# Group B of an attention block: where the score differences live, and when the fp16 pieces are made

## The chip, the cores and the metric

One core of a Trainium2 chip runs the kernel in one launch. The metric is the device time of that launch in microseconds (us). Engines: PE (TensorE matmul; PEld is its weight load), DVE (VectorE), ACT (ScalarE), POOL (GpSimd) and SP (SyncE), which here issues the DMAs. SBUF is the working memory; PSUM is the memory into which matmuls write.

## The reference

One layer, sequence 1024, width 1024, float32:

```python
n = rms_norm(h, norm1_g)
qa, ka, va, qb, kb, vb = split(n @ w_in)
ya = mixer_a(qa, ka, va, sinks)      # 8 heads of 64, 2 K/V heads, window of 3 chunks of 64, ALiBi, sinks
yb = mixer_b(qb, kb, vb, rel_bias)   # 8 heads of 64, own chunk and 8 chunks before it
y = concat(rms_norm(ya, g_a), rms_norm(yb, g_b))
h = h + y @ w_out
h = h + square(relu(rms_norm(h, norm2_g) @ w_ff1)) @ w_ff2
out = rms_norm(h, final_norm_g)
```

mixer_b, which the change touches, is per head: `scores = q k^T / 8 + bias[clipped distance]` over the nine chunks of the band (a key outside it counts -1e30), `softmax` over them, times v.

## The kernel before, in words

The program first projects the first K, Q and V of group A, then does group A's attention, group B's, the output projection with the second norm, and the MLP. Every fp32 product is made from a high and a low piece of its operands.

**Group B.** Queries go in row blocks of 128, keys likewise; row block i sees key blocks max(0, i − 4) to i, so n = 128 to 640 columns. Heads come in pairs j = 0 to 3 (`Pair("B", j, ...)`). A `UnitB` is one head of a pair (s = 0, 1) for one half of the sequence (t = 0, 1; four row blocks). The order is, for each pair, (s0, t0), (s1, t0), (s0, t1), (s1, t1): 16 units, 64 calls of `score`. In units of t = 0 the row blocks have 128, 256, 384 and 512 columns, in units of t = 1 all have 640.

`score(b)` of row block b does, in this order:
- PE: the scores into PSUM tile S (two banks; two such tiles);
- DVE (L554): bias − score, with the row minimum into nm, written back into S. The page calls it CUSTOM_DVE_ANT_0; a second small instruction reads the minimum;
- ACT (L555): the exponential in place in S, with the row sum into sm;
- DVE (L764, L765): scale and reciprocal of the sum, rc;
- ACT (L770): the high fp16 piece, S × rc, into H (SBUF; two such tiles);
- DVE (L771): the low fp16 piece, S × rc − high, into the same H;
- SP (L772): a DMA that transposes H into G (fp16, one per unit; three such tiles, one of pool `at` and two of pool `atB`).

`step`/`apply` of a unit multiplies G by V, key block by key block, into PSUM tile av; a unit of t = 0 has four such steps and needs all four row blocks at the first, one of t = 1 has eight and needs row block 0 at the first, 0 and 1 at the second, and so on. After the last step ACT copies av out (L802, L803), and at s = 1 POOL adds the halves and `finish` makes y.

**Order.** The calls of `score` run two units ahead: while unit u is applied, `interleave` puts the four calls of `score` of unit u + 2 between its steps, and between those `Filler` steps of three matmuls each: the projections of the pairs to come (ip_kB, ip_qB, ip_vB) and at last the output projection of group A's part (op_A). PE's order is fixed by hand in the order of the calls. On the other engines and in the queue of SP, a planner at compile time orders the instructions by its own times and by when tiles come free; each engine then runs its list strictly in that order.

**Biases.** `Pair.biases()` is called in each `score`; its first call in a pair loads both heads' biases (L590, 320 KB each, two tiles `bias`) on SP and has POOL fill two corners of each with -1e30 (L591, L592).

**Pools.** `atA` (six P tiles of group A, 640 columns of fp32) is closed at the first unit of group B, and `atB` (two G tiles) is opened over it. Pool `at` has the biases, three PT tiles, H, one G tile and Y.

Of the kernel before, what the change touches and what calls it, by code (L numbers as in the profile page):

```python
# [17 lines left out]
P = 128  # L18
# [34 lines left out]
def kernel(  # L53
# [61 lines left out]
    small.tile([P, 88], F32, tag="pad", bufs=1, name="pad")  # L115
# [425 lines left out]

    def exponentials(kind, i, bias, init, S, pr, nm, sm):

        k0, n = window(kind, i)
        w = (2 if kind == "A" else 5) * P
        bs = bias[:, w - n : w]
        if kind == "A":
            S, pr = S[:, 0, :n], pr[:, :n]
        elif n > 512:
            S, bs = S[:, :, :320], bs.rearrange("p (a b) -> p a b", a=2)  # L550
            pr = S
        else:
            S = pr = S[:, 0, :n]
        nc.vector.tensor_tensor_reduce(pr, S, bs, -1.0, init, ALU.add, ALU.min, nm)  # L554
        nc.scalar.activation(pr, pr, AF.Exp, bias=nm, scale=-1.0, accum_out=sm)  # L555
        return k0, n, pr
# [12 lines left out]
    class Pair:  # L569
# [7 lines left out]
        def biases(self):  # L577
            if self.kind == "A" and self.j == 0:
                return first_bias
            if self.bias:  # L580
                return self.bias
            for s in range(2):
                h = 2 * self.j + s
                b = at.tile([P, 5 * P], F32, tag="bias", bufs=2, name=f"b_{self.kind}{h}")
                if self.kind == "A":
                    far = b[:, 2 * P : 4 * P]
                    nc.sync.dma_start(far, dist)
                    nc.gpsimd.tensor_scalar(b[:, : 2 * P], far, 2.0 ** -(h + 1), None, ALU.mult)
                else:
                    nc.sync.dma_start(b, relb[h])  # L590
                    nc.gpsimd.memset(b[:HD, 5 * P - HD :], NEG)  # L591
                    nc.gpsimd.memset(b[HD:, :HD], NEG)  # L592
                self.bias.append(b)
            return self.bias

# [57 lines left out]
    class UnitA:  # L653
# [10 lines left out]
        def score(self, s):  # L664
# [4 lines left out]
            pt = atA.tile([P, 5 * P], F32, tag="P", bufs=6, name=f"P_{self.name}_{s}")  # L669
# [21 lines left out]
        def turn(self, u):  # L691
# [4 lines left out]
            T = self.T[u] = at.tile([P, 2, HALF], F32R, tag="PT", bufs=3, name=f"T_{self.name}_{u}")  # L696
# [41 lines left out]
    units_b = [0]  # L738

    class UnitB:  # L740


        def __init__(self, pair, s, t):
# [5 lines left out]
            self.at = {}  # L749

        def score(self, b):
            p, h = self.pair, self.h
            if b == 0:
                self.nm, self.sm, self.rc = stats(self.name)
                bank = banks_of_b()
                n = units_b[0] % 3
                units_b[0] += 1
                pool, bufs = (at, 1) if n == 0 else (group_ps[2], 2)
                self.G = pool.tile([P, 40, P], F16, tag="T16", bufs=bufs, name=f"G_{self.name}")
            c = slice(b, b + 1)  # L760
            S = group_ps[1].tile([P, 2, 512], F32, tag="S", bufs=2, name=f"S_{self.name}_{b}")
            scores("B", self.i0 + b, p.Q[self.s], p.K[self.s :: 2], S)
            k0, n, q = exponentials("B", self.i0 + b, p.biases()[self.s], BIG, S, None, self.nm[:, c], self.sm[:, c])
            nc.vector.tensor_scalar(self.sm[:, c], self.sm[:, c], 2.0**-P_UP, None, ALU.mult)  # L764
            nc.vector.reciprocal(self.rc[:, c], self.sm[:, c])  # L765
            H = at.tile([P, 10 * P], F16, tag="P16", bufs=2, name=f"H_{self.name}_{b}")
            hi, lo = H[:, :n], H[:, n : 2 * n]
            if n > 512:
                hi, lo = (v.rearrange("p (a b) -> p a b", a=2) for v in (hi, lo))
            nc.scalar.activation(hi, q, AF.Copy, scale=self.rc[:, c])  # L770
            nc.vector.scalar_tensor_tensor(lo, q, self.rc[:, c], hi, ALU.mult, ALU.subtract)  # L771
            nc.sync.dma_start_transpose(self.G[:, 10 * b : 10 * b + 2 * n // P], H[:, : 2 * n])  # L772
            self.at[self.i0 + b] = (10 * b - k0, n // P)
# [175 lines left out]
    for j in range(4):  # L949
# [4 lines left out]
        pair = Pair("B", j, Q, K, V, y7 if j == 3 else None)  # L954
        units += [(UnitB(pair, s, t), f"B{j}", B_FILL[4 * j + 2 * t + s]) for t in range(2) for s in range(2)]
# [18 lines left out]
    for unit, name, n_fill in units:  # L974
# [7 lines left out]
        nexts = list(look_ahead(LOOK_AHEAD))  # L982
        interleave(unit, nexts, n_fill, unit.name[0] == "A" and ahead and ahead[-1].name[0] == "B")
# [566 lines left out]
```

## Time and profile before

| | |
|---|---|
| median of 3 runs | 1107.96 us (1103.93 to 1111.24) |
| the profiled execution | 1105.94 us |
| its span, first to last instruction | 1103.7 us |
| granted TensorE clock, mean | 0.983 |
| PE busy | 1038.9 us |
| DVE, ACT, POOL busy | 674.2, 599.2, 429.9 us |
| first score of group B, last product with V | 156.9 us, 425.0 us |

The profile gives for a group of instructions its line, engine, operation, tiles (`out<-in`), shapes and count, then busy us, mean ns of one, and the idle time of the engine just before them with what ended it. A row of waits reads: who waited, for what, us in total, how often, the longest. A row of the timeline reads: start us, length, engine, line, operation, and in brackets the idle time before it and its releaser. A matmul's line is always that of a helper (L165), so products are told apart by their tiles: S_B scores of group B, av_B products with V, op_A the output projection.

### The profile page before, as it was taken

How to read it: one execution, taken by the hardware profiler on the slowest of the kernel's cores; microseconds unless marked ns; L12 is line 12 of the kernel's file. 1: busy time of each engine (PE TensorE's matmuls, PEld its weight loads, DVE VectorE, ACT ScalarE, POOL GpSimd, SP SyncE). 2: the span in 40 equal slices, each digit the busy share in tenths (PEclk: the TensorE clock that was granted, in tenths of full speed). 3: DMA queues.
4: the chain of work that ended last, by engine and by line, in shares of the span. 5: the costliest groups of instructions: out<-in, count | busy, mean ns of one | idle time of the engine just before them, and what ended most of it. 6: DMA issues, size and time to landing. Idle time of an engine off the chain costs nothing.

```text
span 1103.7 us, 14073 instructions
## 1 busy us (share of the span) xinstructions
PE 1038.9 (94%) x4787; PEld 834.9 (76%) x4787; DVE 674.2 (61%) x1108; ACT 599.2 (54%) x1005; POOL 429.9 (39%) x334
## 2 busy tenths in 40 slices
PE   9999988987687987999999999999999999999997
PEld 7888876756455655888888888888888888888885
DVE  6578765646454362588543244334888776778666
ACT  8677776635475584767545444545623333333346
POOL 0567783322352343502644443454114124024125
PEclk9999998999899998999999999999999999999999
DMA  9945456896999678232545354235898545533004
GB/s 359 247 115 149 138 145 161 164 209 121 218 224 261 142 165 253 109 106 94 184 153 177 110 172 172 110 120 210 312 390 311 167 134 170 174 115 96 1 1 153
DMA packets 146119, 187.98 MB, mean 170 GB/s; under 512 B 79744, under 2 KB 97152, under 8 KB 146048
## 3 DMA queue, kind: packets, MB, share of 16 engines
q1 hardware_dynamic: 145904, 186.83, 56.4%
q8 instruction: 38, 0.62, 0.2%
q14 instruction: 33, 0.27, 0.1%
q10 hardware_dynamic: 144, 0.26, 0.1%
HBM read 105.26 MB, written 45.09 MB: 136 GB/s over the span
## 4 chain that ended last, share of the span: by engine, by line
PE 63%; ACT 1%; DVE 1%; DMA 0%; issue 0%; POOL 0%; ACTq 0%; DVEq 0%
PE f L165 28%; PE f_a L165 16%; PE f_c L165 8%; PE op_B L165 4%; PE f_b L165 4%; PE op_A L165 1%; PE tp L168 1%; PE av_B L165 1%; DMA G_B<-H_B 0%; PE S_B L165 0%; ACT H_B L770 0%; DVE H_B L771 0%; PE end L165 0%; ACT yc L803 0%; PE ss_B L165 0%
## 5 line engine op out<-in xcount | busy, mean ns | idle before, releaser
L165 PE MATMUL f<-X,W 128*128 128x512 f32 x1344 | 311.3, 393 | 0.0
L165 PEld LDWEIGHTS f<-X,W 128*128 128x128 f32 x1344 | 252.1, 188 | 57.9 <-DVE X L171 0.4
L165 PE MATMUL f_a<-V,U 128*128 128x512 f32 x756 | 174.9, 390 | 0.0
L171 POOL TENSOR_TENSOR U<-u,U 128x1024 fp32r<-128x1024 f32 x32 | 79.3, 2480 | 230.9 <-PE f_c L165 137.2
L165 PEld LDWEIGHTS f_a<-V,U 128*128 128x128 f32 x756 | 141.9, 188 | 31.1 <-DVE C L1439 0.3
L171 POOL TENSOR_TENSOR W<-T,W 128x1024 fp32r<-128x1024 f32 x29 | 75.5, 2604 | 144.9 <-ACT W L1146 140.2
L165 PE MATMUL S_B<-KkB,QqB 128*128 128x320 f32 (+2 forms) x192 | 48.4, 363 | 43.7 <-DVE H_B L771 37.1
L165 PE MATMUL f_c<-V,U 128*128 128x512 f32 x384 | 89.0, 390 | 0.0
L165 PEld LDWEIGHTS f_c<-V,U 128*128 128x128 f32 x384 | 72.1, 188 | 15.6
L1146 ACT ACTIVATE V<-Z 128x1024 fp32r<-128x1024 f32 x32 | 33.9, 1059 | 90.4 <-PE f_a L165 45.3
L165 PEld LDWEIGHTS S_B<-KkB,QqB 128*128 128x128 f32 x192 | 31.7, 199 | 55.0 <-issue 37.9
L771 DVE SCALAR_TENSOR_TENSOR H_B<-S_B,rc_B,H_B 128x640 f16<-128x640 f32 (+2 forms) x64 | 45.7, 716 | 44.0 <-ACT H_B L770 43.8
L1146 ACT ACTIVATE V<-w 128x1024 fp32r<-128x1024 f32 x24 | 25.5, 1061 | 81.6 <-issue 34.8
L171 DVE TENSOR_TENSOR V<-w,V 128x1024 fp32r<-128x1024 f32 x24 | 50.2, 2090 | 31.0 <-ACT V L1146 31.0
L171 POOL TENSOR_TENSOR W<-w,W 128x1024 fp32r<-128x1024 f32 x23 | 56.4, 2456 | 32.1 <-ACT W L1146 32.0
L1195 DVE TENSOR_TENSOR k<-f,k 128x1024 f32<-128x1024 f32 x24 | 29.3, 1222 | 63.7 <-PE f L165 63.7
L555 ACT ACTIVATE S_B<-S_B,nm_B 128x640 f32<-128x640 f32 (+2 forms) x64 | 40.4, 632 | 49.8 <-DVE nm_B L554 47.4
L1146 ACT ACTIVATE U<-u 128x1024 fp32r<-128x1024 f32 x56 | 58.6, 1046 | 10.3 <-DMA ud<-k 6.5
L554 DVE CUSTOM_DVE_ANT_0 S_B<-S_B,b_B 128x640 f32<-128x640 f32 (+2 forms) x64 | 42.3, 664 | 34.6 <-PE S_B L165 19.7
L770 ACT ACTIVATE H_B<-S_B,rc_B 128x640 f16<-128x640 f32 (+2 forms) x64 | 42.0, 659 | 37.3 <-DMA G_B<-H_B 25.1
L1189 ACT ACTIVATE k<-f 128x1024 f32<-128x1024 f32 x24 | 24.6, 1026 | 62.2 <-PE f L165 62.2
L165 PE MATMUL ip_qB<-nT,w_qB 128*128 128x512 f32 x192 | 53.6, 413 | 0.9 <-DVE ts_kB L359 0.9
(247 smaller groups left out, 1981.7 us busy)
## 6 DMA issues: line engine op xcount, KB each, us to landing
w<-in_w_ff_dram SPq DMA_DIRECT2D x64, 512.0 KB, 4.8
u<-ud SPq DMA_DIRECT2D x56, 512.0 KB, 4.4
ud<-k SPq DMA_DIRECT2D x48, 512.0 KB, 3.0
KkB<-ts_kB SPq DMA_DIRECT2D x64, 128.0 KB, 2.3
yd<-y SPq DMA_DIRECT2D x14, 512.0 KB, 3.2
y<-yd SPq DMA_DIRECT2D x14, 512.0 KB, 6.3
xr<-in_x_dram SPq DMA_DIRECT2D x8, 512.0 KB, 8.6
QqB<-ts_qB SPq DMA_DIRECT2D x32, 128.0 KB, 2.3
```

The costliest lines, as they stand in the source:

```text
L165: pe(nc.tensor.matmul(*args, **kw))
L168: pe(nc.tensor.transpose(*args))
L171: return engine.tensor_tensor(lo, full, f(hi), ALU.subtract)
L554: nc.vector.tensor_tensor_reduce(pr, S, bs, -1.0, init, ALU.add, ALU.min, nm)
L555: nc.scalar.activation(pr, pr, AF.Exp, bias=nm, scale=-1.0, accum_out=sm)
L770: nc.scalar.activation(hi, q, AF.Copy, scale=self.rc[:, c])
L771: nc.vector.scalar_tensor_tensor(lo, q, self.rc[:, c], hi, ALU.mult, ALU.subtract)
L1146: nc.scalar.activation(w[0], full, AF.Copy)
L1189: nc.scalar.activation(kept[p], ps, AF.Copy)
L1195: dve.tensor_tensor(v, ps, v, ALU.add)
```

## The change

- The difference (L554) is written into P, a tile in SBUF (640 columns of fp32, three in pool `at`), no longer back into S; exponential, high and low piece read P. Group A's P tiles are three of `at` and three of `atA`, in turn.
- The pieces of two row blocks are made together and later. `score(b)` first puts the scores on PE, then runs one item of the list `defer`, then makes difference and exponential. After odd b two items are appended for the pair (b − 1, b): `upper` (scale and reciprocal for both columns at once, both high pieces) and `lower` (both low pieces, both transposes). So `upper` runs in the next call of `score`, `lower` in the one after it; for blocks 2 and 3 these are calls of the next unit. What is left is run when no scores are left to come, and before a unit's first product with V.
- H has three tiles. G has two tiles for units of t = 0 (26 columns of 128 each, in `at`) and two for t = 1 (40 columns, in `atB`).
- Biases: unit (s0, t0) loads its pair's second bias in call 1 and fills its corners in call 3; unit (s1, t1) does this for the next pair's first. Pair 0 loads and fills both in its own first call.
- `atA` has the PT tiles now; it is closed, and `atB` opened, at the first unit of t = 1. The small tile `pad` has 8 columns, no longer 88.

```diff
-    small.tile([P, 88], F32, tag="pad", bufs=1, name="pad")
+    small.tile([P, 8], F32, tag="pad", bufs=1, name="pad")
...
-            group_ps.append(ap_.enter_context(tc.tile_pool(name="atB", bufs=1, reuse_waits="tile")))
...
-    atA = group_ps[0].enter_context(tc.tile_pool(name="atA", bufs=1, reuse_waits="tile"))
+    only_a = ExitStack()
+    atA = only_a.enter_context(tc.tile_pool(name="atA", bufs=1, reuse_waits="tile"))
+    only_b = []
+
+    def pool_of_b():
+        if not only_b:
+            only_a.close()
+            only_b.append(ap_.enter_context(tc.tile_pool(name="atB", bufs=1, reuse_waits="tile")))
+        return only_b[0]
+
+    rows_of_a = [0]
+
+    def tile_of_a(name):
+        n = rows_of_a[0]
+        rows_of_a[0] += 1
+        pool, bufs = (atA, 3) if n % 2 else (at, 3)
+        return pool.tile([P, 5 * P], F32, tag="P", bufs=bufs, name=name)
...
-        if kind == "A":
-            S, pr = S[:, 0, :n], pr[:, :n]
-        elif n > 512:
-            S, bs = S[:, :, :320], bs.rearrange("p (a b) -> p a b", a=2)
-            pr = S
+        pr = pr[:, :n]
+        if n > 512:
+            v = lambda a: a.rearrange("p (a b) -> p a b", a=2)
+            nc.vector.tensor_tensor_reduce(v(pr), S[:, :, :320], v(bs), -1.0, init, ALU.add, ALU.min, nm)
         else:
-            S = pr = S[:, 0, :n]
-        nc.vector.tensor_tensor_reduce(pr, S, bs, -1.0, init, ALU.add, ALU.min, nm)
+            nc.vector.tensor_tensor_reduce(pr, S[:, 0, :n], bs, -1.0, init, ALU.add, ALU.min, nm)
         nc.scalar.activation(pr, pr, AF.Exp, bias=nm, scale=-1.0, accum_out=sm)
...
             for s in range(2):
+                if self.kind == "B":
+                    self.load_bias(s)
+                    self.mask_bias(s)
+                    continue
...
+        def load_bias(self, s):
+            h = 2 * self.j + s
+            b = at.tile([P, 5 * P], F32, tag="bias", bufs=2, name=f"b_B{h}")
+            nc.sync.dma_start(b, relb[h])
+            self.bias.append(b)
+
+        def mask_bias(self, s):
+            b = self.bias[s]
+            nc.gpsimd.memset(b[:HD, 5 * P - HD :], NEG)
+            nc.gpsimd.memset(b[HD:, :HD], NEG)
...
-            pt = atA.tile([P, 5 * P], F32, tag="P", bufs=6, name=f"P_{self.name}_{s}")
+            pt = tile_of_a(f"P_{self.name}_{s}")
...
-            T = self.T[u] = at.tile([P, 2, HALF], F32R, tag="PT", bufs=3, name=f"T_{self.name}_{u}")
+            T = self.T[u] = atA.tile([P, 2, HALF], F32R, tag="PT", bufs=3, name=f"T_{self.name}_{u}")
...
-    units_b = [0]
+    defer, pairs_b = [], []
...
             if b == 0:
                 self.nm, self.sm, self.rc = stats(self.name)
-                bank = banks_of_b()
-                n = units_b[0] % 3
-                units_b[0] += 1
-                pool, bufs = (at, 1) if n == 0 else (group_ps[2], 2)
-                self.G = pool.tile([P, 40, P], F16, tag="T16", bufs=bufs, name=f"G_{self.name}")
+                banks_of_b()
+                pool, cols = (pool_of_b(), 40) if self.t else (at, 26)
+                self.G = pool.tile([P, cols, P], F16, tag=f"T16_{self.t}", bufs=2, name=f"G_{self.name}")
             c = slice(b, b + 1)
             S = group_ps[1].tile([P, 2, 512], F32, tag="S", bufs=2, name=f"S_{self.name}_{b}")
+            pt = at.tile([P, 5 * P], F32, tag="P", bufs=3, name=f"P_{self.name}_{b}")
             scores("B", self.i0 + b, p.Q[self.s], p.K[self.s :: 2], S)
-            k0, n, q = exponentials("B", self.i0 + b, p.biases()[self.s], BIG, S, None, self.nm[:, c], self.sm[:, c])
+            if defer:
+                defer.pop(0)[1]()
+            self.P[b] = exponentials("B", self.i0 + b, p.biases()[self.s], BIG, S, pt, self.nm[:, c], self.sm[:, c])
+            if b % 2:
+                self.next_bias(b == 1)
+            if b % 2:
+                H = {}
+                defer.append((self, lambda: self.upper(b - 1, H)))
+                defer.append((self, lambda: self.lower(b - 1, H)))
+
+        def next_bias(self, load):
+            s, j = 1 - self.s, self.pair.j + self.s
+            if self.s != self.t or j in (0, 4):
+                return
+            if load:
+                pairs_b[j].load_bias(s)
+            else:
+                pairs_b[j].mask_bias(s)
+
+        def upper(self, b0, H):
+            c = slice(b0, b0 + 2)
             nc.vector.tensor_scalar(self.sm[:, c], self.sm[:, c], 2.0**-P_UP, None, ALU.mult)
             nc.vector.reciprocal(self.rc[:, c], self.sm[:, c])
-            H = at.tile([P, 10 * P], F16, tag="P16", bufs=2, name=f"H_{self.name}_{b}")
...
-            nc.scalar.activation(hi, q, AF.Copy, scale=self.rc[:, c])
-            nc.vector.scalar_tensor_tensor(lo, q, self.rc[:, c], hi, ALU.mult, ALU.subtract)
-            nc.sync.dma_start_transpose(self.G[:, 10 * b : 10 * b + 2 * n // P], H[:, : 2 * n])
-            self.at[self.i0 + b] = (10 * b - k0, n // P)
+            for b in (b0, b0 + 1):
+                k0, n, q = self.P[b]
+                H[b] = at.tile([P, 10 * P], F16, tag="P16", bufs=3, name=f"H_{self.name}_{b}")
+                nc.scalar.activation(H[b][:, :n], q, AF.Copy, scale=self.rc[:, b : b + 1])
+
+        def lower(self, b0, H):
+            for b in (b0, b0 + 1):
+                k0, n, q = self.P[b]
+                nc.vector.scalar_tensor_tensor(
+                    H[b][:, n : 2 * n], q, self.rc[:, b : b + 1], H[b][:, :n], ALU.mult, ALU.subtract
+                )
+                o = (10 if self.t else 6) * b
+                nc.sync.dma_start_transpose(self.G[:, o : o + 2 * n // P], H[b][:, : 2 * n])
+                self.at[self.i0 + b] = (o - k0, n // P)
...
             if first:
+                while any(q[0] is self for q in defer):
+                    defer.pop(0)[1]()
...
         nexts = list(look_ahead(LOOK_AHEAD))
+        while defer and not nexts:
+            defer.pop(0)[1]()
```

More of the change, by code (lines that the diff above doesn't have):

```diff
@@ L582, in biases @@
             for s in range(2):
+                if self.kind == "B":
+                    self.load_bias(s)
+                    self.mask_bias(s)
+                    continue
                 h = 2 * self.j + s
                 b = at.tile([P, 5 * P], F32, tag="bias", bufs=2, name=f"b_{self.kind}{h}")
[L585 to L592, printed above, removed]
+                far = b[:, 2 * P : 4 * P]
+                nc.sync.dma_start(far, dist)
+                nc.gpsimd.tensor_scalar(b[:, : 2 * P], far, 2.0 ** -(h + 1), None, ALU.mult)
                 self.bias.append(b)
             return self.bias
+        def load_bias(self, s):
[7 more added lines that the diff above has]
+            nc.gpsimd.memset(b[HD:, :HD], NEG)
         def rows(self, t):
@@ L748, in __init__ @@
             self.second = [lambda n=n: self.step(n) for n in range(len(self.kbs))]
-            self.at = {}
+            self.at, self.P = {}, {}
         def score(self, b):
@@ L954 @@
         pair = Pair("B", j, Q, K, V, y7 if j == 3 else None)
+        pairs_b.append(pair)
         units += [(UnitB(pair, s, t), f"B{j}", B_FILL[4 * j + 2 * t + s]) for t in range(2) for s in range(2)]
```

3 lines of the change are left out of this document (removed).

## The prediction

> **What bounds the kernel now.** I read the page's busy shares first, then busy time by stretch (columns: length, then busy us and count of PE, PEld, DVE, ACT and POOL, granted clock, DMA share, GB/s), cut where group B's first score and the last group B product lie.
>
> ```profile
> PE 1038.9 (94%) x4787; PEld 834.9 (76%) x4787; DVE 674.2 (61%) x1108; ACT 599.2 (54%) x1005; POOL 429.9 (39%) x334
> 0.00:156.00 156.00, 154.15 (x808) 129.25 (x809) 110.78 (x316) 118.82 (x311) 90.69 (x106) 1.00 0.63 190
> 156.00:290.00 134.00, 113.59 (x543) 86.29 (x542) 76.15 (x214) 75.93 (x147) 49.61 (x63) 0.96 0.79 172
> 290.00:412.00 122.00, 96.28 (x456) 68.21 (x455) 59.21 (x170) 74.26 (x149) 45.77 (x50) 0.94 0.85 202
> 412.00:426.00 14.00, 4.84 (x18) 2.40 (x17) 2.56 (x5) 6.42 (x13) 8.34 (x13) 0.63 1.07 310
> 426.00:1103.70 677.70, 670.06 (x2970) 548.79 (x2968) 425.48 (x405) 323.74 (x388) 235.50 (x104) 1.00 0.45 157
> ```
>
> TensorE bounds the whole, but not evenly. Before 156 us and after 426 us it is all but full at clock 1.00. In the 270 us of group B it is busy 113.59 + 96.28 + 4.84 = 214.7 us, so 55.3 us are idle, and only there can this change act. Next, PE's waits and its longest gaps in the timeline:
>
> ```profile
> PE S_B L165 <- DVE H_B L771: 37.1, 17, 7.6
> PE av_B L165 <- DMA G_B<-H_B: 9.2, 2, 7.5
> PE S_B L165 <- DVE sm_B L764: 5.3, 5, 1.7
> 166.32 0.98 PE L165 MATMUL S_B<-KkB,QqB 128*128 128x384 f32 x2 [4.05 <-DVE H_B L771]
> 264.62 1.29 PE L165 MATMUL S_B<-KkB,QqB 128*128 128x320 f32 x4 [3.89 <-DVE H_B L771]
> 298.87 0.98 PE L165 MATMUL S_B<-KkB,QqB 128*128 128x384 f32 x2 [7.62 <-DVE H_B L771]
> 355.39 1.40 PE L165 MATMUL S_B<-KkB,QqB 128*128 128x320 f32 x4 [4.83 <-DVE H_B L771]
> 419.67 0.80 PE L165 MATMUL av_B<-G_B,VvB 128*128 128x384 f16 x2 [7.47 <-DMA G_B<-H_B]
> ```
>
> A score product waits for the low piece H (L771) of the row block two calls earlier: that is the last reader of its PSUM tile S, which has two buffers. This costs 37.1 + 5.3 = 42.4 us. Of the 17 waits on L771 four make 20.4 us; the other thirteen average 1.3 us. The 9.2 us stand at the end of the stage, where the last unit's transposes must land.
>
> Why L771 is late, in DVE's and ACT's waits:
>
> ```profile
> DVE H_B L771 <- ACT H_B L770: 43.8, 37, 3.7
> DVE sm_B L764 <- ACT S_B L555: 33.6, 42, 2.1
> DVE S_B L554 <- POOL b_B L591: 13.3, 2, 8.9
> ACT H_B L770 <- DMA G_B<-H_B: 25.1, 17, 3.7
> ```
>
> DVE and ACT hand each block back and forth, ACT also waits for an H buffer that a transpose still reads, and twice the first difference of a pair waits for its bias; the longer of these, 8.9 us, is what ends in the 7.62 us gap.
>
> **The change, part by part.** The durations at the widest block (640 columns), the same operations where they already use SBUF (group A's P_A, and y), and last the start of the first difference (164.1):
>
> ```profile
> L554 DVE CUSTOM_DVE_ANT_0 S_B<-S_B,b_B 128x640 f32<-128x640 f32 x32 | 26.6, 830 | 11.3 <-PE S_B L165 11.1
> L554 DVE DVE_READ_ACCUMULATOR2_ANT nm_B<- 128x1 f32 x64 | 9.1, 142 | 0.0
> L555 ACT ACTIVATE S_B<-S_B,nm_B 128x640 f32<-128x640 f32 x32 | 24.5, 764 | 15.9 <-DVE nm_B L554 13.8 <-DVE sm_B L764 2.0
> L555 ACT ACTIVATION_READ_ACCUMULATOR S_B<-S_B,nm_B 128x1 f32 x64 | 12.5, 195 | 0.0
> L764 DVE TENSOR_SCALAR sm_B<-sm_B 128x1 f32<-128x1 f32 x64 | 9.7, 152 | 34.3 <-ACT S_B L555 33.6
> L765 DVE RECIPROCAL rc_B<-sm_B 128x1 f32<-128x1 f32 x64 | 10.4, 163 | 1.9
> L770 ACT ACTIVATE H_B<-S_B,rc_B 128x640 f16<-128x640 f32 x32 | 25.4, 792 | 18.3 <-DMA G_B<-H_B 7.8 <-DVE nm_B L554 3.8 <-issue 2.8
> L771 DVE SCALAR_TENSOR_TENSOR H_B<-S_B,rc_B,H_B 128x640 f16<-128x640 f32 x32 | 28.2, 882 | 18.4 <-ACT H_B L770 18.4
> L554 DVE CUSTOM_DVE_ANT_0 P_A<-S_A,b_A,nsink 128x256 f32<-128x256 f32 x56 | 25.2, 479 | 4.9 <-PE S_A L165 4.7
> L554 DVE CUSTOM_DVE_ANT_0 S_B<-S_B,b_B 128x256 f32<-128x256 f32 x8 | 3.5, 439 | 1.1 <-PE S_B L165 1.1
> L555 ACT ACTIVATE P_A<-P_A,nm_A 128x256 f32<-128x256 f32 x56 | 28.1, 503 | 12.0 <-DVE nm_A L554 11.9
> L555 ACT ACTIVATE S_B<-S_B,nm_B 128x256 f32<-128x256 f32 x8 | 3.5, 443 | 3.1 <-DVE nm_B L554 3.1
> L771 DVE SCALAR_TENSOR_TENSOR H_B<-S_B,rc_B,H_B 128x512 f16<-128x512 f32 x8 | 6.0, 748 | 6.6 <-ACT H_B L770 6.6
> L816 DVE SCALAR_TENSOR_TENSOR y<-Y,gain_vB,y x8: 743/752/1177, 219.9 to 428.7; 128x512 fp32r<-128x512 f32 x8
> L554 DVE CUSTOM_DVE_ANT_0 S_B<-S_B,b_B x64: 289/756/833, 164.1 to 409.8; 128x640 f32<-128x640 f32 x32, 128x128 f32<-128x128 f32 x8, 128x256 f32<-128x256 f32 x8, 128x384 f32<-128x384 f32 x8
> ```
>
> *Early release of S.* Now a PSUM tile is held for 0.83 + 0.14 + 0.76 + 0.20 + 0.15 + 0.16 + 0.79 + 0.88 = 3.9 us after its score. 64 calls over 214.7 us are 3.4 us a call, so PE wants the tile back 6.7 us later, less 0.7 us for the score: about 2 us of slack, and every delay beyond that stops PE. Afterwards PE needs only the difference: 0.97 us, slack 5 us. The next ring is P, three SBUF tiles: the difference of block 3 takes the tile of block 0, and stands on DVE behind the pair's two low pieces. The loop from block 1's difference is 0.97 + 0.96 + 0.31 + two high pieces 1.58 + a low piece 0.88 + 0.97 = 5.7 us, and PE asks for the result four calls (13.4 us) later: slack 7 us. So some 3 us are gained on every wait. That erases the thirteen short ones and leaves about 1 and 2 us of those of 3.89 and 4.83.
>
> *Biases one unit ahead.* The same eight loads and sixteen small fills, moved ahead on SP and POOL. Three calls (10 us) lie between load and use, and a bias lands in 3.3 to 5.2 us (below), so the 7.62 us go. The very first pair still loads both at once: its first difference starts at 164.1 us and S is free by 164.5 instead of 166.3, so of 4.05 us some 2 stay. On POOL a fill can stand behind another wait; then the difference and the score two calls on wait too. I keep that in the remainder.
>
> *Cost of SBUF.* Exponent: 503 against 443 ns, 0.06 × 64 = 4 us more on ACT. Difference: 479 against 439, 2.5 us on DVE. The high piece's price from SBUF at this width stands in no row; between nothing and the exponent's 0.06, I take 0.03, so 2 us more of ACT. Scale and reciprocal go from 64 to 32 each: DVE saves 32 × 0.315 = 10 us. All this is hidden as long as ACT (75.93 + 74.26 + 6.42 = 156.6 us now, 163 then) keeps room in a stage of some 239 us: 68%.
>
> *Low piece with two SBUF inputs.* y (L816) already has this form: its median of 752 ns equals the 748 ns from PSUM, its longest is 1177. I take no extra cost. The Trainium skill, page "SBUF — State Buffer", section "Who interferes with whom", says that a VectorE instruction with two SBUF inputs contends with a GpSimd instruction that reads SBUF; the median of L816 doesn't show it, its maximum may. If each of the 64 paid as the longest did, it would be 64 × 0.43 = 27 us of DVE.
>
> *Pieces in pairs, later.* The transposes leave one to two calls later. What is late next is the product with V:
>
> ```profile
> L772 SPq DMA_TRANSPOSE G_B<-H_B x64: 1167/1342/4923, 168.0 to 416.7; - x64
> DMA to landing us min/median/max: 2.3/3.5/9.4
> DMA to landing us min/median/max: 3.3/4.3/5.2
> 377.42 0.50 PE L165 MATMUL S_B<-KkB,QqB 128*128 128x256 f32 x2 [0.72 <-DVE H_B L771]
> 386.47 0.61 PE L165 MATMUL av_B<-G_B,VvB 128*128 128x512 f16 x2
> 265.71 4.08 PE L165 MATMUL ip_kB<-nT,w_kB 128*128 128x512 f32 x12
> 280.80 2.89 PE L165 MATMUL ip_qB<-nT,w_qB 128*128 128x512 f32 x12
> ```
>
> (First landing row: transposes; second: biases.) A unit's last low pieces will be issued in block 1 of the next unit, as at 377.42, and a first-half unit needs all its blocks at its first product, as at 386.47: 9 us. Needed: two low pieces 1.5, two issues 2.7, landing 3.5, together 7.7 us; with the longest landing 13.6. So mostly hidden; 2 us in total. Queued behind on SP are the copies of K and Q, wanted a pair later. A third H buffer eases ACT's 25.1 us.
>
> *End of the stage.* No score follows the last pair; two high and two low pieces in a row instead of one are 0.8 + 0.9 us longer, partly against ACT work now in between: 9.2 becomes 10 us.
>
> *Clock.* After a long gap matmuls run slower: twelve took 4.08 us instead of 2.89 behind the 3.89 us gap. At 1.2 us for each of the five gaps shown that makes 6; 4 go with their gaps, one stays with that of the end.
>
> *Pools moved.* Group A keeps six P and three PT tiles; PE's 154.15 of 156 us covers that stage. Nothing; if not, 0 to 2 us.
>
> The remainder: everything else must run in the shorter stage. DMA is 0.79 × 134 + 0.85 × 122 + 1.07 × 14 = 225 us, 94% of a stage of 239 us and 101% of one of 223 us, where every wait would be gone; the highest share above is 1.07. Transposes will queue longer, and delays now hidden add up. Besides 2 + 3 us I let 7 us of the waits stay: 42.4 − 12 = 30 us go.
>
> **Sum,** on the profiled execution (span 1103.7, 1105.94 with what lies around it): −30 − 4 + 2 + 1 = −31, so 1075; the median of the runs is 2 us above that execution: **1077 us**.
>
> **The rivals.**
> 1. *All waits go:* 42.4 + 6 − 1 = 47 us, 1061; for it the low averages of DVE and ACT, against it DMA. Chance 0.10.
> 2. *DMA or ACT paces the second half.* From 290 to 412 us PE idles 122 − 96.28 = 25.7 us, 18 of them beside the bias gap; DMA has 0.85 × 122 = 104 us there, so without the 25.7 us its share would be 1.08. If the 18 us stay, 42.4 − 18 − 4 = 20 us of waits go and 2 of the clock, and 3 come back: 1089. Chance 0.20.
> 3. *Nothing gained:* the P ring takes over from S, because the planner's order on DVE and ACT puts a wait ahead of each difference; or fills stuck on POOL give back the bias gain. The 43.8 and 33.6 us of DVE waits speak for it, the computed slack against. 1108 ± 8. Chance 0.10.
> 4. *DVE pays for the shared reads:* 27 us, all on the loop: 1104. In the skill's terms this is the rule above at its worst. Chance 0.03.
> 5. *Slower: products with V wait for late transposes.* Each of the 16 units waits. It decides from 31 / 16 = 1.9 us a unit; at 3.5 us (one landing) it is 56 − 31 = 25 us, 1133. For it: landings up to 9.4 us and fuller DMA; against: 9 us of lead. Chance 0.09.
>
> **Numbers.** The forecast has 0.48 (1066 to 1085). Under 1% (11 us) this kernel's measurement, which spread over 7 us, tells no change. Faster by over 1%: 0.48 + 0.10 + 0.20 = 0.78; within: 0.13; slower: 0.09. For 8 in 10 the range takes in rivals 1 and 2 with their unknowns: 1056 to 1100.
>
> **What would show it.** Right: PE's wait S_B on the low piece gone or under 10 us, what remains naming the difference; stretches 156 on at clock 0.98 or more; DVE's wait on the bias only in the first pair; the end wait near 10 us; DMA share near 1. Wrong: av_B waiting for G in the middle of the stage (rival 5), L771's mean well over 0.9 us at 640 columns (4), DVE waits moved ahead of L554 (3), ACT waits on H as long as now (2).

## The result, and the profile after

The changed kernel takes **1077.41 us** (median of 4 runs, 1075.00 to 1078.07) against 1108.62 us for the kernel before (4 runs, 1103.93 to 1111.24): ratio 0.9719, 95% interval 0.9682 to 0.9756. The profiled execution took 1077.9 us with a span of 1076.1 us; before, 1105.94 and 1103.7. One execution of the version with y first (below) took 2654.92 us against 1071.61 to 1072.78 us of its other three and is left out of its median.

The first rows to compare are TensorE's own stretches (columns: length, PE's busy us and count of matmuls, granted clock, DMA share, GB/s). Group B is cut at its last product with V, which ends at 425.3 us before and at 406.1 us after. Before, from 290 us on:

```profile
290.00:425.30 135.30, 100.42 (x469) 0.91 0.87 213
425.30:500.00 74.70, 74.70 (x368) 1.00 0.36 129
500.00:1103.70 603.70, 596.06 (x2606) 1.00 0.46 161
```

After, from group B's start:

```profile
156.00:290.00 134.00, 120.71 (x596) 0.99 0.84 187
290.00:406.10 116.10, 86.60 (x412) 0.87 0.93 229
406.10:480.00 73.90, 73.84 (x362) 0.99 0.36 130
480.00:1076.10 596.10, 589.85 (x2613) 1.00 0.47 163
```

With the prediction's row for 156 to 290 us (113.59 busy), group B (from 156 us on) is 269.3 us before, of which PE works 214.0 and idles 55.3. After, it is 250.1 us: 207.3 of work, 42.8 idle. So group B is 19.2 us shorter, 12.5 of it idle time and 6.7 less time at work for nearly the same matmuls (1010 records and 1006). The remaining 8.4 us of the span's 27.6 come **behind** group B: 678.4 us before and 670.0 after, in a part of the program whose instructions the change doesn't touch. There the multilayer perceptron (first to last of its matmuls) takes 7.8 us less, 609.4 instead of 617.2, and what follows it 1.3 less (the same with the pad at 88 below, so not by the pools; not explained); the output projection takes 0.7 more.

PE's waits after the change (engine, first reader, what ended the wait: us in total, times, longest):

```profile
PE av_B L165 <- DMA G_B<-H_B: 22.4, 10, 6.8
PE op_A L165 <- DMA y<-yd: 8.8, 1, 8.8
PE S_B L165 <- DVE nm_B L567: 6.2, 4, 2.5
PE S_B L165 <- DVE nm_B L565: 1.4, 2, 1.2
```

The score's wait on the low piece is gone. Of its 42.4 us, 7.6 stay, and they name the difference (L565 and L567). In their place the product with V waits 22.4 us (9.2 before), and group A's output projection, which waited 0.7 us for y before, now waits 8.8. Five of the gaps, from the timeline (start, length, operation; the gap in brackets):

```profile
163.76 0.59 PE L165 MATMUL S_B<-KkB,QqB 128*128 128x384 f32 x2 [2.24 <-DVE nm_B L567]
313.54 4.56 PE L165 MATMUL op_A<-w_o,y 128*128 128x512 f32 x9 [8.82 <-DMA y<-yd]
393.47 0.27 PE L165 MATMUL av_B<-G_B,VvB 128*128 128x128 f16 x2 [3.70 <-DMA G_B<-H_B]
394.49 0.58 PE L165 MATMUL av_B<-G_B,VvB 128*128 128x256 f16 x2 [0.75 <-DMA G_B<-H_B]
401.90 0.80 PE L165 MATMUL av_B<-G_B,VvB 128*128 128x384 f16 x2 [6.83 <-DMA G_B<-H_B]
```

The last three rows and 0.28 us at 402.98 are the end of the stage: 11.6 us. The other 10.8 us of the 22.4 lie in its middle.

Why y is late is read from SyncE's queue of DMA issues around that gap:

```profile
295.56 5.19 SPq L820 DMA_TRANSPOSE G_B<-H_B  x3
301.51 0.33 SPq L121 DMA_DIRECT2D st_o<-in_w_out_dram  x1
304.39 3.87 SPq L820 DMA_TRANSPOSE G_B<-H_B  x3
308.36 2.01 SPq L897 DMA_DIRECT2D y<-yd  x4
```

The four y loads are issued at 308.4 us, behind transposes and loads of output weights (`st_o`, into a stage buffer) that stand ahead of them in the same queue. Between 286 and 316 us the queue's transposes wait 7.6 us for low pieces (L816), its weight loads 1.1 us for POOL, which reads the stage buffers. The first y load lands at 313.4 us, 5 us after its issue.

The durations that the change touches (group B's stretch, each shape apart; busy us, then mean ns of one):

```profile
L816 DVE SCALAR_TENSOR_TENSOR H_B<-P_B,rc_B,H_B 128x640 f16<-128x640 f32 x32 | 31.6, 1012 | 24.0 <-ACT H_B L811 23.8
L565 DVE CUSTOM_DVE_ANT_0 P_B<-S_B,b_B 128x640 f32<-128x640 f32 x32 | 26.1, 819 | 13.5 <-PE S_B L165 13.1
L806 DVE TENSOR_SCALAR sm_B<-sm_B 128x2 f32<-128x2 f32 x32 | 10.1, 314 | 22.1 <-ACT P_B L568 22.1
L568 ACT ACTIVATE P_B<-P_B,nm_B 128x640 f32<-128x640 f32 x32 | 26.4, 825 | 19.2 <-DVE nm_B L565 12.3 <-DVE top_vB L400 2.5 <-DVE e_vB L401 2.5
L811 ACT ACTIVATE H_B<-P_B,rc_B 128x640 f16<-128x640 f32 x32 | 25.2, 818 | 6.5 <-DMA G_B<-H_B 3.5 <-issue 1.4 <-DVE rc_B L807 1.0
```

Exponent 764 to 825 ns, high piece 792 to 818, difference 830 to 819, low piece 882 to 1012, scale 152 to 314.

### The profile page after: what moved, and what is told of

It reads as the page before. It is cut to its first block, busy times and chain, and to the rows that moved or that the text cites. A ratio compares the mean times of both kernels' runs of the same rounds, so it can differ in the third digit from the quotient of the medians.

```text
span 1076.1 us, 14044 instructions
## 1 busy us (share of the span) xinstructions
PE 1025.3 (95%) x4787; PEld 833.1 (77%) x4787; DVE 677.4 (63%) x1044; ACT 601.0 (56%) x1005; POOL 439.2 (41%) x334
## 4 chain that ended last, share of the span: by engine, by line
PE 80%; DMA 6%; ACT 5%; DVE 4%; issue 2%; POOL 1%; SPq 1%; ACTq 0%; DVEq 0%; POOLq 0%
PE f L165 27%; PE f_a L165 16%; PE f_c L165 8%; PE op_B L165 4%; PE f_b L165 4%; PE ip_qA L165 4%; DMA G_B<-H_B 4%; PE op_A L165 3%; PE ip_vB L165 2%; PE ip_kB L165 2%; PE ip_qB L165 2%; PE S_B L165 1%; PE av_B L165 1%; PE S_A L165 1%; PE ip_kA L165 1%
## 5 line engine op out<-in xcount | busy, mean ns | idle before, releaser
L165 PE MATMUL f<-X,W 128*128 128x512 f32 x1344 | 306.0, 389 | 0.1
L171 POOL TENSOR_TENSOR U<-u,U 128x1024 fp32r<-128x1024 f32 x32 | 80.0, 2499 | 227.3 <-PE f_c L165 135.2
L816 DVE SCALAR_TENSOR_TENSOR H_B<-P_B,rc_B,H_B 128x640 f16<-128x640 f32 (+2 forms) x64 | 54.9, 873 | 43.1 <-ACT H_B L811 42.6
L165 PE MATMUL av_B<-G_B,VvB 128*128 128x512 f16 (+3 forms) x192 | 43.8, 320 | 22.6 <-DMA G_B<-H_B 22.4
L1199 ACT ACTIVATE U<-u 128x1024 fp32r<-128x1024 f32 x56 | 58.5, 1044 | 10.1 <-DMA ud<-k 7.0
L568 ACT ACTIVATE P_B<-P_B,nm_B 128x640 f32<-128x640 f32 (+2 forms) x64 | 44.2, 691 | 35.3 <-DVE nm_B L567 13.8
L165 PE MATMUL op_A<-w_o,y 128*128 128x512 f32 x192 | 52.0, 409 | 8.8 <-DMA y<-yd 8.8
L811 ACT ACTIVATE H_B<-P_B,rc_B 128x640 f16<-128x640 f32 (+2 forms) x64 | 42.0, 686 | 21.2 <-DMA G_B<-H_B 15.8
```

The lines of the kernel that those rows point to most:

```text
L165: pe(nc.tensor.matmul(*args, **kw))
L171: return engine.tensor_tensor(lo, full, f(hi), ALU.subtract)
L811: nc.scalar.activation(H[b][:, :n], q, AF.Copy, scale=self.rc[:, b : b + 1])
L816: nc.vector.scalar_tensor_tensor(H[b][:, n : 2 * n], q, self.rc[:, b : b + 1], H[b][:, :n], ALU.mult, ALU.subtract)
L1199: nc.scalar.activation(w[0], full, AF.Copy)
```

## The experiments

Two questions: which part of the change brings and which costs the 19.2 us in group B, and what brings the 8.4 us behind it. In the multilayer perceptron behind group B the matmuls stand back to back, so their distance can be read off stretches without a gap. Before, then after:

```profile
510.00:740.00 230.00, 230.00 (x997) 1.00 0.44 151
850.00:1020.00 170.00, 170.00 (x745) 1.00 0.45 146
```

```profile
510.00:740.00 230.00, 230.00 (x1016) 1.00 0.45 155
850.00:1020.00 170.00, 170.00 (x752) 1.00 0.38 120
```

At an equal clock of 1.00, 19 and 7 more matmuls fit. From the starts of single matmuls, they stand 231.1 ns (510 to 740) and 228.9 ns (850 to 1020) apart before, 226.7 ns in both after. What the change moves there is only addresses: with the pad at 88 numbers the pools of the later stages begin at byte 168384 of each partition, with 8 at byte 168064 (worked out from the tiles' addresses in the two programs).

**The pad alone.** The kernel before, with one line changed:

```
-    small.tile([P, 88], F32, tag="pad", bufs=1, name="pad")
+    small.tile([P, 8], F32, tag="pad", bufs=1, name="pad")
```

> The kernel before with the small tile pad at 8 columns instead of 88, so that every pool opened after it starts 320 bytes per partition lower; nothing else changes. After group B the changed kernel's profile is 8.4 us shorter than that of before, with 226.7 ns between matmuls of the MLP instead of 231.1 and 228.9. Theory 'place': the start of the later pools sets the spacing of the matmuls that read them, so this kernel has 226.7 ns in the MLP, its stretch after group B is about 670 us, and it is 8 us (5 to 11) faster than before, about 0.75%. Rival 'spread': the 8.4 us are the difference of two profiled executions, so the spacing stays near 231 and 229 ns and the time within 3 us of before.

Measured: 1102.16 us, ratio 0.994 (0.9921 to 0.996), and the distance of the changed kernel:

```profile
510.00:740.00 230.00, 230.00 (x1016) 1.00 0.43 151
```

The reverse, the changed kernel with the pad back at 88:

> The changed kernel with the small tile pad back at 88 columns, so that its later pools start where those of before do. Theory 'place': the MLP has 231 and 229 ns between matmuls again, and the kernel is about 8 us slower than the changed one, near 1086 us, 22 us faster than before. Rival 'spread': no difference from the changed kernel, about 1077 us.

Measured: 1085.78 us, ratio 0.98 (0.9781 to 0.9818), with the old distance:

```profile
510.00:740.00 230.00, 230.00 (x997) 1.00 0.42 147
PE av_B L165 <- DMA G_B<-H_B: 21.9, 10, 6.7
```

PE's waits on G stay as they were, and the time rises by 8.4 us. So the place of the pools is worth 8.4 us in the changed kernel by the medians. By the profiles the multilayer perceptron alone takes 7.8 us less with the pad of 8 in both pairs (617.2 and 609.4 us). In the kernel before the medians moved by 5.5 us only: its profiled execution lost 3.9 us in group B (last product with V ends at 429.2 us, not 425.3). There PE is idle as long (55.2 and 55.3 us) but at work for 218.0 us in place of 214.0, and the granted clock is lower (0.84 in place of 0.92 from 156 to 200 us, 0.91 in place of 0.96 from 250 to 290). Why this version gets the lower clock is open.

**The early release alone.** The changed kernel without pairs and without deferral (the biases ahead, the third H tile, the new G tiles and the place of the pools stay); each block's scale, pieces and transpose follow its own exponential again:

```
-            if defer:
-                defer.pop(0)[1]()
...
-            if b % 2:
-                H = {}
-                defer.append((self, lambda: self.upper(b - 1, H)))
-                defer.append((self, lambda: self.lower(b - 1, H)))
+            H = {}
+            self.upper(b, H)
+            self.lower(b, H)
```

`upper` and `lower` then work on one block instead of two.

> The changed kernel without the deferral and the pairs: each block's scale, reciprocal, pieces and transpose are issued in its own call, as before, but from the SBUF tile P, with S freed by the difference. Theory 'release': the early release of S alone takes PE's waits for S from 42 us to under 15 us, and as transposes leave one to two calls earlier, the waits of the products with V fall from 22.4 us to about 10 us (the end alone): time within 6 us of the changed kernel, 1071 to 1083 us. Rival 'deferral': without it the differences stand on DVE behind each block's wait for ACT, so S is held nearly as long as before: PE's waits for S 25 us or more, time 1088 to 1100 us.

Measured: **1072.68 us**, ratio 0.9682 (0.9664 to 0.97).

```profile
PE op_A L165 <- DMA y<-yd: 10.7, 2, 10.5
PE av_B L165 <- DMA G_B<-H_B: 8.5, 4, 5.0
PE S_B L165 <- DVE nm_B L567: 8.1, 3, 5.3
```

The score waits no longer than in the changed kernel (8.1 us against 7.6), and the product with V waits 8.5 us for G instead of 22.4 (2.1 us more name an exponential). Pairs and deferral together cost 4.7 us of the median and bought nothing that shows in a wait of the scores.

**Without the bias one unit ahead.** The changed kernel without the call that loads and fills it ahead, so that both biases of a pair are loaded at its start:

```
-            if b % 2:
-                self.next_bias(b == 1)
```

> The changed kernel with both biases of a pair loaded and filled in the pair's first call of score, as before. Theory 'bias hidden by the early load': without it the first differences of pairs 1 to 3 wait 4 to 9 us each for the bias, S is not freed, and 5 to 12 us come back: 1082 to 1090 us. Rival 'the bias was one accident': only one pair lost time on it before, the rings behind it now absorb the wait, and the time stays within 3 us of the changed kernel.

Measured: 1082.71 us, ratio 0.9768 (0.9747 to 0.9788).

```profile
PE S_B L165 <- DVE nm_B L567: 16.9, 3, 8.6
PE av_B L165 <- DMA G_B<-H_B: 15.3, 10, 6.1
```

Gaps of 8.64 us (ending at 286.0 us) and 6.01 us (at 354.4 us) stand where a pair's first difference waits for its bias. Net of the shorter waits of the product with V, the earlier load is worth 5.3 us.

**y before the output weights.** The changed kernel, with one order turned round in `out_proj_a`:

```
         ys, ws = [], []
         for m in range(4):
-            ws.append(out_weight(m))
-        for m in range(4):
             ys.append(load_y(m, (0,)))
+        for m in range(4):
+            ws.append(out_weight(m))
```

> The changed kernel with one thing moved: the output projection issues its four loads of y ahead of the loads of its weights, so that on the queue of the synchronising engine they stand before loads that wait for stage buffers. Theory 'queue': the new wait of 8.8 us of op_A for y (at 313.5 us in the changed kernel) exists because these loads stood behind the weights' loads; it falls under 2 us, and the time is 1068 to 1071 us. Rival 'behind the transposes': the loads stand behind the last transposes of H_B whatever their order among the loads, the wait keeps 5 us or more and the time is 1074 to 1078. Rival 'another wait': the wait for y goes, but a wait for o, for the weights or of pt takes its place, 1073 to 1078.

Measured: 1071.83 us, ratio 0.9675 (0.9659 to 0.9692). The wait for y is gone, but only 5.6 us of its 8.8 are gained. The time lies 0.8 us above the queue theory's range: the rival "another wait" has a part. PE's wait, SyncE's queue before it, and PE and the DMA engines while it lasts:

```profile
PE av_B L165 <- ACT w_o L223: 7.8, 1, 7.8
```

```profile
292.58 1.96 SPq L897 DMA_DIRECT2D y<-yd  x4
294.60 1.23 SPq L121 DMA_DIRECT2D st_o<-in_w_out_dram  x2
295.92 6.22 SPq L820 DMA_TRANSPOSE G_B<-H_B  x2
302.24 1.28 SPq L121 DMA_DIRECT2D st_o<-in_w_out_dram  x1
```

```profile
298.50:306.30 7.80, 0.01 (x1) 0.75 1.09 359
```

The product with V needs no output weight; the split that the row names (L223, which makes a weight's high piece from its stage buffer) merely ended at the same moment. PE stands at the semaphore of the second transpose of the 6.22 us row, which lands at 306.04 us, and goes on at 306.29. Both transposes of that row were issued ahead of the weight's load at 302.24 and landed late, at 305.01 and 306.04 us: the four y loads and two weights issued before them landed one after another, from 297.27 to 304.25, with the DMA engines busy throughout (share 1.09). So the y loads now stand ahead of what the product with V needs. That the data ahead of them is what held the transposes is read from the order of the landings; no run tests it by itself.

The same order in the version with the early release only:

> The version with only the early release (no pairs, nothing deferred) and the y loads ahead of the output weights' loads. Theory 'queue': its wait of op_A for y was 10.7 us; that goes under 2 us, and the time falls from 1072.7 to 1062 to 1065 us, below every version so far. Rivals as for the changed kernel with this order: 5 us or more of the wait stay, or another wait takes its place, 1068 to 1073.

Measured: 1073.38 us, ratio 0.9684 (0.9667 to 0.9701): no gain over 1072.68.

```profile
PE op_A L165 <- ACT w_o L223: 4.3, 2, 3.6
PE op_A L165 <- ACT o L982: 3.8, 1, 3.8
PE op_A L165 <- POOL w_o L171: 2.3, 2, 1.3
```

Here the rival is right: in place of the wait for y there are waits of 6.6 us for the weights, and that for o (ACT's copy of the projection's result) is 3.8 us, 3.1 before.

**Where the pools may stand.** Two more bases for the changed kernel, 64 and 128 bytes up:

> The changed kernel with the pad at 24 numbers in place of 8: the later pools begin 64 bytes higher, at byte 168128 of each partition, which is an odd multiple of 64. Theory 'boundary of 128 bytes': the matmuls of the multilayer perceptron stand about 229 to 231 ns apart in place of 226.7, and the time is 1083 to 1087 us. Rival 'distance' (the further up, the slower, so that 64 of 320 bytes bring a fifth): spacing 227.5 ns, 1078 to 1080. Rival 'something else of the pad of 88': 226.7 ns, 1077.

> The changed kernel with the pad at 40 numbers in place of 8: the later pools begin 128 bytes higher, at byte 168192, again a multiple of 128 (and of 256). Theory 'boundary of 128 bytes': spacing 226.7 ns in the multilayer perceptron, time 1075 to 1079 us. Rival 'same place within 1024 bytes as the main pool' (which the pad of 8 gives and this one does not): 229 to 231 ns, 1083 to 1087. Rival 'distance': 228.5 ns, 1080 to 1081.

Measured: 1086.55 us, ratio 0.9806 (0.979 to 0.9823), and 1086.67 us, ratio 0.9806 (0.9791 to 0.9821). The first agrees with a boundary of 128 bytes, the second refutes it: byte 168192 is a multiple of 128 and yet slow.

```profile
510.00:740.00 230.00, 230.00 (x997) 1.00 0.43 150
```

That left the rival, the same place as the main pool within some power of two. I put each matmul of the perceptron in this last run beside the addresses of its two operands (the stationary block and the 512 streamed columns). The main pool's pages begin 128 bytes behind a multiple of 256, the later pools at a multiple of 256:

| stationary operand in | streamed operand in | matmuls | mean distance to the next |
|---|---|---|---|
| main | main (next block in main) | 658 | 226.8 ns |
| later pool | later pool | 773 | 227.3 ns |
| later pool | main | 388 | 233.3 ns |
| later pool (of the first half) | main | 422 | 234.1 ns |

So with this offset of 128 bytes a matmul takes about 7 ns more when its two operands lie at different places within 256 bytes, and 5.7 ns more in 424 others, whose own operands are in main but whose successor's stationary block lies in the later pool (232.5 ns). With the offset of 64 bytes (the kernel before) the pattern is less clean: 235.8 ns with the stationary block in the later pool of the first half and the streamed operand in main, but also 227.8 to 228.8 ns where both lie in one pool. What is shown is thus the effect of how the pools lie to each other, not a price of each matmul by its own operands. Two kernels tell the remaining theories apart: 256 bytes up, and 64 bytes ahead of the main pool, so that all pools move together:

> The changed kernel with the pad at 72 numbers in place of 8: the later pools begin 256 bytes higher, at byte 168320, at the same distance from a multiple of 256 as the main pool's pages (128 bytes for both), but not from a multiple of 512 (384 against 128). Theory 'same place within 256 bytes': spacing 226.7 ns in the multilayer perceptron, 1075 to 1079 us. Rival 'same place within 512 bytes or more': 229 ns or more on the matmuls whose two operands lie in different pools, 1083 to 1087. Rival 'distance': 231 ns, 1084 to 1087.

```
     ident = cp.tile([P, P], F32, name="ident")
+    cp.tile([P, 16], F32, name="pad0")
```

> The changed kernel with 64 bytes put ahead of the main pool, so that the main pool's pages and the later pools all begin 64 bytes higher (bytes 1216 and 168128) and keep their relation. Theory 'relation' (both operands of a matmul in the same place within 256 or 512 bytes): spacing 226.7 ns and 1075 to 1079 us, although the later pools stand at the very byte at which they cost 9 us with the pad of 24. Rival 'absolute place' (only an odd multiple of 128 bytes is fast): 229 to 231 ns, 1083 to 1087 us.

Measured: 1077.1 us, ratio 0.9703 (0.968 to 0.9727), and 1077.14 us, ratio 0.9709 (0.9681 to 0.9736). A row of the second:

```profile
510.00:740.00 230.00, 230.00 (x1016) 1.00 0.45 157
```

Both are as fast as the changed kernel, the second with its later pools at byte 168128, where they cost 9 us while the main pool stood elsewhere. Of the offsets tried (0, 64, 128, 256 and 320 bytes), those that agree within 256 bytes are fast: the relation decides, not the place.

**Pairs without deferral.** The changed kernel, with the two blocks' pieces made right behind the second exponential:

```
-            if defer:
-                defer.pop(0)[1]()
...
-                defer.append((self, lambda: self.upper(b - 1, H)))
-                defer.append((self, lambda: self.lower(b - 1, H)))
+                self.upper(b - 1, H)
+                self.lower(b - 1, H)
```

> The changed kernel with its pairs but without deferral: high and low pieces of two blocks are made right behind the exponentials of the second. Theory 'deferral': the 4.7 us between the changed kernel and the version with only the early release come from making the pieces one and two calls late; without it the waits of the products with V on the transposes fall from 22.4 to 8 to 12 us and the time is 1071 to 1074 us. Rival 'pairs' (the first block waits for the second, and two low pieces follow each other): the waits stay at 18 us or more and the time is 1076 to 1079. Rival 'both in part': 1074 to 1076.

Measured: 1073.75 us, ratio 0.9674 (0.9649 to 0.9699), 3.4 us under the two runs above, which were on the same chip.

```profile
PE av_B L165 <- DMA G_B<-H_B: 11.5, 6, 6.3
PE op_A L165 <- DMA y<-yd: 11.3, 1, 11.3
```

The waits of the products with V are half those of the changed kernel (11.5 us, not 22.4). The scores wait 11.5 us there (7.6 in the changed kernel) and op_A 11.3 (8.8), which takes part of it back. It is the deferral that costs, not the pairs; against the early release alone (1072.68 us, on another chip) pairs bring nothing measurable either.

**y between the weights.** The early release alone, with the y loads behind three of the four weights:

```
         for m in range(4):
+            if m == 3:
+                for n in range(4):
+                    ys.append(load_y(n, (0,)))
             ws.append(out_weight(m))
-        for m in range(4):
-            ys.append(load_y(m, (0,)))
```

> The version with only the early release, and the four loads of y put behind three of the four loads of the output weights instead of behind all four: the first three find a free stage buffer at once, the fourth waits. Theory 'the first of the two that is late sets the start': op_A then waits for the fourth weight in place of y and starts at 308 to 311 us in place of 313.1, the time is 1069 to 1072 us. Rival 'no gain': what is saved there comes back at the next wait, for o on the scalar engine, 1072 to 1074.

Measured: **1070.1 us**, ratio 0.9644 (0.9615 to 0.9672), the lowest median of all.

```profile
306.75 1.62 PE L165 MATMUL op_A<-w_o,y 128*128 128x512 f32 x3 [6.27 <-DMA y<-yd]
336.69 2.93 PE L165 MATMUL op_A<-w_o,y 128*128 128x512 f32 x6 [4.17 <-ACT o L983]
```

op_A starts at 306.75 us, 6.4 us earlier than with the early release alone (313.13) and earlier than I expected; what it waits for is still y. The time is in the range of the first theory, but the rival has its part: the wait for o rose from 3.1 to 4.2 us, and 2.6 us of the 6.4 reach the median. The two were measured on different chips, on which the kernel before had medians of 1107.65 and 1110.99 us, so the size of these 2.6 us is uncertain.

## Why the prediction was right, and where it was not

The total, 1077 against 1077.4, came out right; its composition did not, and that the two agree so closely is luck. With the pad back at 88, where only the parts act to which the prediction gave a price, the time is 1085.78 us, just above its range of 1066 to 1085. The sum for group B was −31 us. Group B gave −19.2, and the stretch behind it, priced at nothing, gave −8.4. That is −27.6 on the profiled executions; the medians differ by 31.2, because the profiled execution before was 2.7 us below its median and the one after 0.5 us above.

| step | predicted | in the traces |
|---|---|---|
| waits of the score for S | −30 | −34.8 |
| product with V, middle of the stage | +2 | +10.8 |
| end of the stage | +1 | +2.4 |
| PE's time at work in group B (predicted: the clock) | −4 | −6.7, of it about 2.6 by the clock |
| group A's output projection waits for y | no term | +8.1 |
| other gaps (the difference to −12.5 idle) | no term | +1.0 |
| pools moved (the multilayer perceptron) | 0, at most 2 | −7.8 |
| the rest behind group B | no term | −0.6 |

**Early release: right.** The prediction said that slack on S goes from 2 to 5 us, so the short waits vanish and the difference becomes the last reader. The six waits that stay name it. 12 us were to stay; 7.6 did. The first bias gap kept 2.24 us where "some 2" was said. That the gain needs neither pairs nor deferral is shown by the version without them. It is 36 us faster than the kernel before; less 5.3 for the biases and 8.4 for the pools, some 22 us are left (an estimate from the three medians). That these are the release's, and not the third H tile's or the new G tiles', is read from the waits: no run has those without the release.

**Biases ahead: right in size.** The price was the 7.62 us gap; taking the edit out cost 5.3 us of the median, net of other waits. "Only in the first pair" was too strong: DVE's wait on the bias fell from 13.3 to 6.6 us, in five places.

```profile
DVE P_B L567 <- POOL b_B L616: 6.6, 5, 4.4
```

**Pieces later: the mis-sized term.** The prediction set 7.7 us of work against 9 us of lead, called 13.6 us the case of the longest landing, and took 2 us. But the sum was made of medians of landing and issue, and these hardly moved (issue 1.34 to 1.36 us, landing 3.5 to 3.6, the rows below); the gaps are made by the few that are late. Each of the gaps in the middle ends with the landing of a transpose. The two longest, 3.66 us ending at 302.64 and 3.05 at 357.61, make 6.7 of the 10.8 us; their transposes landed 5.5 and 8.1 us after their issue, against a median of 3.6. The next, 1.78 us at 271.20, ends with one that landed in 3.4 us but was issued late.

```profile
L820 SPq DMA_TRANSPOSE G_B<-H_B x64: 1169/1355/6697, 167.2 to 397.3; - x64
DMA to landing us min/median/max: 2.3/3.6/10.9
```

That without deferral these waits halve (11.5 us) shows that making the pieces later is what uncovers them. Rival 5's mechanism thus came true at 13 us in the whole stage, far below the 31 at which it would have decided.

**What stands behind the transposes: missed.** The prediction named the copies of K and Q as what stands behind the transposes on SyncE's queue. It did not follow the queue to the loads of y, whose late issue is a wait of 8.8 us. The versions with another order show that cause, and also how little of it can be had: 5.6 us in the changed kernel, nothing or 2.6 us with the early release alone.

**Pools moved: wrong.** I looked only for a tile that group A might lack. The address itself was the effect: it changes the distance of 2,676 matmuls (1344 + 756 + 384 + 192 by the groups of the profile) by 2 to 4 ns. The 1344 at 4.1 ns (230.9 to 226.8) and the other 1332 at 1.9 are 8.0 us, close to the 7.8 measured.

**Prices of SBUF.** The exponent's +0.06 us (764 to 825 ns) and the high piece's +0.03 (792 to 818) came as taken; the difference got no dearer (830 to 819). The low piece is dearer than taken: 882 to 1012 ns. The trace tells why. At 640 columns, 14 low pieces that no GpSimd elementwise instruction overlaps average 882 ns, as before; 18 that one overlaps average 1113. The longest:

```profile
267.50 1.90 DVE L816 SCALAR_TENSOR_TENSOR H_B<-P_B,rc_B,H_B 128x640 f16<-128x640 f32 x1 [2.82 <-ACT H_B L811]
267.42 1.29 POOL L171 TENSOR_TENSOR ts_kB<-ts_kB 128x512 fp32r<-128x512 f32 x1
```

GpSimd's instruction began at 267.42, VectorE's at 267.50, which took 1.90 − 0.88 = 1.02 us longer than those not overlapped, most of GpSimd's 1.29. This is what the Trainium skill, page "SBUF — State Buffer", section "Who interferes with whom", says of a VectorE instruction with two SBUF inputs, and the trace agrees; before, with one input in PSUM, the low piece took 882 ns in both cases. In all it is 54.9 us of low pieces instead of 45.7, 9.2 us and not the 27 of rival 4, and VectorE's slack hid it: with it in place, the score waits were shorter than predicted.

**DMA and clock.** DMA share rose to 0.93 in group B's second half, as said; rival 2's sign (ScalarE's wait for H as long as before) did not show, 15.8 us against 25.1. The clock was said to be 0.98 or more from 156 us on; it was 0.99 up to 290 us and 0.87 behind that, where the long gaps are now. The term of −4 us was that matmuls behind a long gap run faster once the gap is gone. In the traces the granted clock is one half during 34 us of group B before and after alike; PE works 21.8 us of these before and 16.6 after, because more of them now fall into gaps, so about 2.6 us (half the difference, an estimate) is what the clock gives. The other 4 us of the 6.7 are not explained; the pools have at most 0.8 of them (PE is at work for 208.1 us with the pad back at 88).

## What to carry to other kernels

Release the scarce buffer early, and stop there: making its follow-up work later as well took back 4.7 us, because the products with V then waited 22.4 us for their transposes in place of 8.5. Price a moved step by its late cases, not by medians, and follow the queue that issues it to its end before pricing what stands behind it at nothing. Hold a wait's named releaser against what the reader needs: one named here was an engine that ended at the moment when two transposes had landed. Where a change moves pool addresses, compare the distance of back-to-back matmuls in a stage that the change doesn't touch.

## What the runs showed of the hardware that I had not expected

Back-to-back matmuls with 512 fp32 columns stood 226.7 ns apart when all pools of their operands began at the same place within 256 bytes of the partition, and on average 229 to 231 ns apart over a stretch when they did not (bases moved by 64, 128 and 320 bytes; by 0 and 256 it cost nothing). The granted clock was the same. What in the chip causes it, no run here shows.

A scale of two columns (L806, 128x2) took 167 ns alone and 560 on average (at most 1.11 us) under a GpSimd elementwise instruction, while the scale of one column before took 151 and 154 ns.

```profile
L806 DVE TENSOR_SCALAR sm_B<-sm_B x32: 149/169/1109, 164.7 to 393.2; 128x2 f32<-128x2 f32 x32
L764 DVE TENSOR_SCALAR sm_B<-sm_B x64: 141/154/155, 165.0 to 412.5; 128x1 f32<-128x1 f32 x64
```

The 32 scales take 10.1 us where 64 took 9.7, so of the 10 us that the prediction took off VectorE for scales and reciprocals only those of the reciprocals (10.4 to 5.3) came. Like the low piece's price, this lay under other work.
